# A hybrid decoder step on one core: conv gate columns last, parts split in place, taps held back in the memory projection, a paced layer norm

## The chip, the cores and the metric

The kernel runs on one core of one Trainium2 chip. The metric is device time in microseconds (us), the median of several runs; one further execution was taken with the hardware profiler. A difference of under about 2% between two kernels is called "same". Engines are named as in the profile: PE is the matmul engine, PEld its weight loads, DVE the vector engine, ACT the scalar engine, POOL the general engine, SP the engine whose queue issues all of this kernel's DMAs.

## The reference

One layer for two groups with the same weights: a prompt (1 sequence of 1024 tokens) and samples (8 sequences of 8 tokens with earlier state). All in float32, d_model 2048.

```python
def hybrid_layer(x, ...):
    proj = jnp.einsum("bld,de->ble", x, w_in)
    glu_a, glu_b, conv_gate, qkv, dn_gate, beta_in, decay_in, mem_q, mem_gate = jnp.split(proj, splits, axis=-1)

    u = glu_a * jax.nn.sigmoid(glu_b)                                   # conv group, 512 channels
    hc, conv_state = causal_dwconv(u, conv_prev, conv_w)                # width 31
    hc = layer_norm(hc + conv_b.astype(dt), conv_ln_g, conv_ln_b)
    out_conv = (jax.nn.silu(hc) * jax.nn.silu(conv_gate)).astype(dt)

    qkv_c, qkv_state = causal_dwconv(qkv, qkv_prev, qkv_conv_w)         # deltanet group, 8 heads of 128
    ...
    o, s_final = gated_delta_rule(q, k, v, g, beta, s0)
    ...
    scores = jnp.einsum("blhd,bmhd->bhlm", mq, mem_k.astype(dt)).astype(f32) * (MEM_HEAD_DIM ** -0.5)
    p = jax.nn.softmax(scores, axis=-1).astype(dt)                      # memory group, 4 heads of 128, 256 tokens
    om = jnp.einsum("blhm,bmhd->blhd", p, mem_v.astype(dt)).reshape(b, l, MEM_WIDTH)
    out_mem = (om * jax.nn.silu(mem_gate)).astype(dt)

    mixed = jnp.concatenate([out_conv, out_dn, out_mem], axis=-1)
    h = jnp.einsum("ble,ed->bld", mixed, w_out)
    y = layer_norm(DEEPNORM_ALPHA * x + h, ln_g, ln_b)
    return y, conv_state, qkv_state, s_final
```

The prompt's memory keys and values are themselves projected from `mem_prompt` (256 x 2048) with `w_mem_k` and `w_mem_v`; the samples bring cached ones.

## The kernel before, in words

**Precision.** Every large matmul is done in three: an operand is split into a high part (rounded to FP32R by an ACT copy) and a low part (DVE: operand minus high part), and `mm3` adds high x high, high x low and low x high. `split_quarter` does this for the weights, a piece of 128 x 512 at a time: ACT writes `wh`, DVE writes `wl`, each from 4 rotating buffers; `ensure(2)` keeps two pieces split ahead of PE in program order. So every piece of weights needs one ACT copy and one DVE subtraction before PE can use it. `put_mixed` (L570) does the same for each finished 128-channel block of the mixed output and writes both parts to DRAM.

**Stages.** Pass 0 takes the first 512 prompt tokens and the 64 sample tokens (moving sizes 288 + 288), pass 1 the other 512 prompt tokens. Each pass runs over 52 columns of `w_in` (128 channels each, `gemm`): 96 matmuls a column in pass 0, 48 in pass 1. `ct_order` gives their order: 32 columns of the deltanet group head by head, eight of the GLU (a and b by turns), then four conv gates (columns 40 to 43), four memory queries (44 to 47), four memory gates (48 to 51). In pass 0, before column 44, `run_mem` projects the memory: 192 matmuls, 32 pieces of weights and 8 of the memory (`load_mem`) to split. In pass 1 `reload_mem` reads the keys and values back at the same column. Then the output phase: `mixed` times `w_out` in blocks of 16 pieces of weights, four column blocks for the first half (`g` = 0, five token tiles, 14 matmuls a piece) and four for the second (`g` = 1, four tiles, 12 matmuls a piece); the last block is cut in two.

**Side work.** Everything else is written as generators (`gen_k`, `gen_chain`, `gen_s`, `gen_cgroup`, `gen_cln`, `gen_att`, `gen_ln` ...). `Side.tick` is called between the matmuls of a column (after every four calls of `mm3`, in pass 1 after every two), in the projection and in the output phase once a piece, and moves each generator on by a step when the planner's clocks (`Model`, one for each engine) say that the tiles it waits for are ready. The program order on each engine is fixed by this planner when the kernel is built; on the chip each engine then goes through its instructions in that order. `Side.drain` calls `tick` until a condition holds, with no column matmuls between. A generator that yields "B" is put off to the next tick.

**Room.** Side work takes its tiles from a pool of 20 `W` tiles; `room(n)` puts a generator off until `n` are free, and `need()` drains until one is. The eviction of a gate column (`gate` in `finish`) calls `need()` and holds its tile until the product that uses it. `gen_att` takes three tiles for a head, and in pass 0 five more for the sample group, whose cached keys and values it loads (`kts`, `vts`). `gen_att` waits for the head before it and, at the end, for its gate.

**The conv group.** `gen_cgroup` (L1020) makes `u` = a x sigmoid(b) and then the 31 taps on DVE, one or two instructions a tap (prompt, samples); a tap waits while the planner's DVE clock is over 1200 ns ahead of its PE clock (L1062). Once all four channel blocks are done, `gen_cln` does the layer norm over channels: sums on POOL, two sums over partitions on PE, then for each block a product with `rstd`, Silu, the product with the gate (it waits for `("g", j)`) and `put_mixed`.

**The end.** After 13 pieces of the first output block `open_out` drains all side work, closes the work pool and opens the pool of the output phase: eight `y` tiles, six `xt`, the layer norm's weights. `residual` (DVE) evicts a bank after each block, `gen_ln` takes statistics after each block and, after the fourth, normalises in four chunks: ACT scales and shifts, DVE multiplies by `lng` and adds `lnb`, SP writes the chunk. After the first block of the second half a drain of all side work (L1689) makes sure that the first half's layer norm is written out before its `y` buffers are taken again.

All recorded operations go through the one helper line 88 (`Proxy`), so the profile's groups are told apart by their tiles: `m` is a column's result, `mm` the memory projection's, `om` the output phase's (and a head's output), `ps` side work on PE, `hc` the conv taps and layer norm, `smz` and `pt` the softmax, `held` the last six pieces of `w_out`.

## Time and profile before

| what | value |
|---|---|
| runs | 4051.27, 2019.34, 2021.03 us; median 2021.03 |
| profiled execution, own time | 2022.13 us |
| its span (first to last instruction) | 2020.4 us |
| mean granted PE clock | 0.992 |
| PE busy | 1964.0 us, 97% |
| DVE busy | 1374.2 us, 68% |
| ACT busy | 922.5 us, 46% |
| conv taps: first of pass 0, last of pass 1 | 585.8 us, 1526 us |
| memory projection, first to last matmul | 715 to 764 us |

The prediction quotes four kinds of views. A *page* line gives an engine's busy time; its row of 40 digits cuts the span in 40 slices (9 is 90% or more). The *waits* say which engine's which tile waited for whom: us in total, how often, the longest. A *stretch* row gives start:end, length, then busy time and instructions of the engines, the granted PE clock, the DMA share and GB/s; a stretch asked for one tile alone counts that tile's instructions only. The *order of time* gives start, duration, engine, operation, output <- inputs, how many were merged, and in brackets the idle time before it and whom it waited for.

### The profile page before, as it was taken

What the parts mean: (1) busy time and instruction counts of PE and PEld (TensorE: products, weight loads), DVE (VectorE), ACT (ScalarE), POOL (GpSimd) and SP (SyncE); (2) the same over time, 40 slices, a digit from 0 to 9 for tenths busy, and PEclk for the clock granted to TensorE, in tenths of its full rate; (3) what the DMA queues carried; (4) which work ended last, traced back from release to release, by engine and by line L of the source; (5) the groups of instructions that cost most, each with busy time, mean ns of one, the idle gap of its engine ahead of it and who ended that gap; (6) DMA issues with size and microseconds to landing.
All of it is one profiled execution on the core that took longest, in us unless ns stands there. A gap on an engine that the chain in (4) does not pass through costs nothing.

```text
span 2020.4 us, 33329 instructions
## 1 busy us (share of the span) xinstructions
PE 1964.0 (97%) x12172; PEld 1710.7 (85%) x12172; DVE 1374.2 (68%) x3423; ACT 922.5 (46%) x2279; POOL 159.9 (8%) x345
## 2 busy tenths in 40 slices
PE   8999999999999999899999999999999999999995
PEld 7999999999999979877888878888887788887784
DVE  6677767866878896455767777778995433338447
ACT  6555555555543244466545544553324522215124
POOL 6111101101101001000000000000101000000001
PEclk9999999999999999999999999999999999999998
DMA  6232333233323354374333333333332493376444
GB/s 209 85 110 74 100 110 110 73 102 110 102 95 101 99 183 131 110 231 150 120 97 99 100 99 106 110 100 95 101 115 77 139 375 103 102 245 206 140 132 150
DMA packets 114294, 257.35 MB, mean 127 GB/s; under 512 B 35281, under 2 KB 39633, under 8 KB 113873
## 3 DMA queue, kind: packets, MB, share of 16 engines
q1 hardware_dynamic: 114128, 255.22, 39.2%
q8 instruction: 96, 1.57, 0.3%
q14 instruction: 70, 0.57, 0.1%
HBM read 219.15 MB, written 36.01 MB: 126 GB/s over the span
## 4 chain that ended last, share of the span: by engine, by line
PE 44%; DVE 6%; issue 1%; ACT 1%; DMA 1%; SPq 0%; POOL 0%; DVEq 0%; ACTq 0%
PE m L88 22%; PE om L88 17%; PE ps L88 5%; DVE y L88 2%; DVE hc L88 1%; DVE wl L88 1%; DVE cv L88 1%; SPq L88 0%; DMA vts<-in_cv_dram 0%; ACT wh L88 0%; DMA ysc<-Y 0%; DVE held L88 0%; DMA mx<-mxl 0%; DMA out_y_p_dram<-y 0%; ACT gmh L88 0%
## 5 line engine op out<-in xcount | busy, mean ns | idle before, releaser
L88 PE MATMUL m<-x,wh 128*128 128x288 f32 (+1 forms) x4992 | 1228.1, 335 | 7.8 <-ACT wh L88 7.8
L88 PEld LDWEIGHTS m<-x,wh 128*128 128x128 f32 x4992 | 833.0, 189 | 84.2 <-issue 16.7
L88 PE MATMUL m<-x,wl 128*128 128x288 f32 (+1 forms) x2496 | 818.4, 328 | 1.7 <-DVE wl L88 1.7
L88 DVE TENSOR_TENSOR wl<-raw,wh 128x512 fp32r<-128x512 f32 x586 | 405.2, 698 | 294.5 <-ACT wh L88 285.6
L88 ACT CAST wh<-raw 128x512 fp32r<-128x512 f32 x586 | 357.3, 620 | 374.3 <-PE om L88 228.2
L88 PEld LDWEIGHTS m<-x,wl 128*128 128x128 f32 x2496 | 470.0, 188 | 37.4 <-DVE wl L88 2.9
L88 PE MATMUL om<-wh,x 128*128 128x512 f32 x1064 | 335.0, 391 | 0.0
L88 PEld LDWEIGHTS om<-wh,x 128*128 128x128 f32 x1064 | 200.7, 189 | 42.7 <-issue 1.0
L88 PE MATMUL om<-wl,x 128*128 128x512 f32 x564 | 220.8, 391 | 3.8 <-DVE wl L88 3.8
L88 DVE SCALAR_TENSOR_TENSOR hc<-u,cvc,hc 128x512 f32<-128x512 f32 x360 | 200.7, 595 | 2.4
L88 DVE TENSOR_TENSOR xt<-mb,X 128x8 f32<-128x8 f32 (+30 forms) x496 | 136.9, 276 | 10.5
L88 DVE SCALAR_TENSOR_TENSOR cv<-xr,qcw,cv 128x512 f32<-128x512 f32 (+1 forms) x216 | 128.9, 597 | 7.7
L88 PEld LDWEIGHTS om<-wl,x 128*128 128x128 f32 x564 | 106.5, 189 | 26.4 <-DVE wl L88 4.4
L88 ACT ACT_TABLE_LOAD x83 | 106.5, 1283 | 44.2 <-DVE smz L88 30.1
L88 DVE TENSOR_REDUCE X<-xt 128x4 f32<-128x8 f32 (+30 forms) x496 | 110.2, 222 | 10.6
L88 ACT ACTIVATE oi<-ps,GT 128x128 f32<-128x128 f32 x56 | 20.6, 368 | 210.1 <-DVE r L88 207.7
L88 ACT ACTIVATE jk<-ps 128x128 f32<-128x128 f32 x128 | 33.3, 275 | 51.8 <-PE ps L88 51.7
L88 ACT COPY xr<-m 128x288 f32<-128x288 f32 (+3 forms) x96 | 33.3, 396 | 20.5 <-PE m L88 20.0
L88 ACT ACTIVATE cv<-cv 128x512 f32<-128x512 f32 x48 | 30.3, 631 | 19.5 <-DVE cv L88 19.2
L88 PEld LDWEIGHTS ps<-S,cv 128*128 128x128 f32 x224 | 32.0, 190 | 4.7 <-DVE S L88 2.2
L88 PE MATMUL ps<-S,cv 128*128 128x128 f32 x224 | 34.4, 276 | 1.1 <-DVE S L88 1.1
L88 DVE SCALAR_TENSOR_TENSOR y<-xt,om 128x512 f32<-128x512 f32 (+1 forms) x36 | 24.2, 682 | 16.4 <-PE om L88 13.7
(318 smaller groups left out, 1817.4 us busy)
## 6 DMA issues: line engine op xcount, KB each, us to landing
raw<-in_wt_dram SPq DMA_DIRECT2D x208, 512.0 KB, 3.8
raw<-in_wo_dram SPq DMA_DIRECT2D x72, 512.0 KB, 3.9
x<-mx SPq DMA_DIRECT2D x16, 576.0 KB, 8.2
mb<-ysc SPq DMA_DIRECT2D x128, 64.0 KB, 2.2
mx<-mxh SPq DMA_DIRECT2D x32, 256.0 KB, 4.8
mx<-mxl SPq DMA_DIRECT2D x32, 256.0 KB, 4.9
xt<-in_xp_dram SPq DMA_DIRECT2D x32, 256.0 KB, 4.4
x<-mx SPq DMA_DIRECT2D x16, 512.0 KB, 3.6
```

Of the source, the lines that this page charges most:

```text
L88: r = fn(**kw)
```

## The change

1. `ct_order`: the four conv gate columns go to the end of each pass (columns 48 to 51); memory queries are now 40 to 43, memory gates 44 to 47. The memory projection and its loads (pass 0) and `reload_mem` (pass 1) move from column 44 to column 40.
2. `put_mixed`: the low part is written over the input tile; one new tile in place of two.
3. The limit by which taps may run ahead of PE becomes a variable: 1200 ns as before, but -500 while `run_mem` puts out its matmuls.
4. `gen_ln`: each chunk's two DVE instructions wait while the planner's DVE clock is over 1200 ns ahead of PE.
5. After the first block of the second half the drain waits only for the first token tile's `gen_ln` of the first half, not for all side work.

```diff
@@ ct_order
-    order += [COL_CGATE + j for j in range(4)]
     order += [COL_MQ + j for j in range(4)]
     order += [COL_MGATE + j for j in range(4)]
+    order += [COL_CGATE + j for j in range(4)]
@@ the order of loads, the column loops of both passes
-        if t == 44:
+        if t == 40:
@@ put_mixed
         yield (m,)
-        yield from room(2)
-        parts = [W([P, NTOK[p]], F32R, name=n, held=True) for n in ("mxh", "mxl")]
-        act.copy(out=parts[0], in_=m)
-        dve.tensor_tensor(out=parts[1], in0=m, in1=parts[0].bitcast(F32), op=ALU.subtract)
-        fr()
-        yield tuple(parts)
+        yield from room(1)
+        hi = W([P, NTOK[p]], F32R, name="mxh", held=True)
+        act.copy(out=hi, in_=m)
+        parts = (hi, m.bitcast(F32R))
+        dve.tensor_tensor(out=parts[1], in0=m, in1=hi.bitcast(F32), op=ALU.subtract)
+        yield (hi, m)
@@ gen_cgroup
+    ahead = [1200]
-            while md.clk["DVE"] > md.clk["PE"] + 1200:
+            while md.clk["DVE"] > md.clk["PE"] + ahead[0]:
                 yield "B"
@@ run_mem
+        ahead[0] = -500
         for i in range(8):
             if i % 2 and i < 7:
                 load_mem()
...
+        ahead[0] = 1200
         need(4)
@@ the pass 0 loop
-        fin = gemm(0, t, fin, refill_b if t == 51 else (lambda q: load_mem() if q == 2 else None) if t == 43 else None)
+        fin = gemm(0, t, fin, refill_b if t == 51 else (lambda q: load_mem() if q == 2 else None) if t == 39 else None)
@@ gen_ln
             act.activation(out=yc, in_=yc, func=AF.Identity, scale=r, bias=nmr)
             yield
+            while md.clk["DVE"] > md.clk["PE"] + 1200:
+                yield "B"
             dve.tensor_tensor(out=yc, in0=yc, in1=gc, op=ALU.mult)
@@ the output phase
             if g and cb == 0:
-                side.drain(lambda: side.q)
+                side.drain(lambda: any(e[0] is first for e in side.q))
...
                     side.add(gen_ln(P, cb, st, ys[i], bst[i], O["y_p"][g * 512 + o:g * 512 + o + P, :]))
+                    if i == 0:
+                        first = side.q[-1][0]
```

## The prediction, as it was put on record

> **What bounds the kernel now.** I read the page first, then the waits of PE, then stretches of 50 us, then the order of time around each stretch that has a hole. The page says that PE is busy nearly all the time at nearly the full clock:

> ```profile
> PE 1964.0 (97%) x12172; PEld 1710.7 (85%) x12172; DVE 1374.2 (68%) x3423; ACT 922.5 (46%) x2279; POOL 159.9 (8%) x345
> PE   8999999999999999899999999999999999999995
> PEclk9999999999999999999999999999999999999998
> ```

> Of the 2020.4 us of the span, 56.4 are without a matmul. A good part lies in the start and the tail (the 8 and the 5 at the row's ends), which the change leaves alone or only reorders. What is left is in the waits of PE (us in total, times, longest):

> ```profile
> PE ps L88 <- DVE pt L88: 6.8, 4, 3.2
> PE om L88 <- DVE wl L88: 3.8, 1, 3.8
> PE ps L88 <- DVE ut L88: 3.4, 5, 1.4
> PE mm L88 <- DVE wl L88: 3.0, 3, 1.4
> PE om L88 <- DVE held L88: 2.6, 3, 1.0
> PE ps L88 <- DMA kts<-in_ckT_dram: 1.5, 2, 0.9
> ```

> No edit takes a matmul away, so the change can only win back waits, and what follows from a wait. That second thing is seen in the stretches (length, then busy time of PE, PEld, DVE, ACT, POOL, then granted clock):

> ```profile
> 800.00:850.00 50.00, 44.65 (x312) 40.30 (x311) 20.30 (x30) 20.82 (x35) 4.28 (x3) 0.93 0.35 111
> 1550.00:1600.00 50.00, 46.83 (x195) 36.19 (x193) 23.44 (x43) 25.88 (x52) 3.88 (x3) 0.93 0.19 63
> 1650.00:1700.00 50.00, 50.00 (x221) 40.95 (x220) 17.51 (x27) 10.56 (x17) 0.00 (x0) 1.00 0.51 171
> 1850.00:1900.00 50.00, 46.25 (x193) 37.74 (x192) 31.44 (x50) 14.31 (x23) 0.00 (x0) 0.93 0.56 178
> ```

> The three stretches with a hole of over 2.5 us have a clock of 0.93; an undisturbed one has 1.00. A mean of 0.93 over 50 us is 0.07 x 50 = 3.4 us of work lost to half speed, on top of the wait itself. So each long wait costs its length plus about 3.4 us.

> **Part 1: gate columns last, memory projection at column 40.** The hole at 840, PE in order of time, with the one ACT row that matters:

> ```profile
> 835.66 1.20 PE L88 MATMUL ps<-kts,dgq 128*32 128x256 f32 x4 [0.58 <-DMA kts<-in_ckT_dram]
> 837.82 1.74 PE L88 MATMUL ps<-kts,dgq 128*32 128x256 f32 x12 [0.95 <-DMA kts<-in_ckT_dram]
> 842.79 0.66 PE L88 MATMUL ps<-ident,pt 128*128 128x128 f32 x2 [3.23 <-DVE pt L88]
> 843.96 1.94 PE L88 MATMUL ps<-vts,ptm 128*32 128x256 f32 x16 [0.52 <-DVE ptm L88]
> 846.71 0.69 PE L88 MATMUL m<-x,wh 128*128 128x288 f32 x2
> 851.94 0.42 PE L88 MATMUL m<-x,wh 128*128 128x288 f32 x2
> 840.29 1.28 ACT L88 ACT_TABLE_LOAD   x1 [8.22 <-DVE smz L88]
> ```

> Scores, softmax and values of one head follow each other with no column's matmul between. I read that as a drain: the eviction of a memory gate asks for a tile (`need` in `gate`), none of the 20 W tiles is free, and the planner puts out side work until one is. By the code, 16 tiles are then held by things that wait: four conv gates, four conv outputs, four memory queries, four tiles of memory keys and values; a head of the sample group needs up to five more. Waits: 0.58 + 0.95 + 3.23 + 0.52 = 5.3; with the clock (0.69 against 0.42 for the same pair of matmuls) 3.4 more: 8.7 us. With the gates last, four of the 16 aren't there when the first heads run, and the heads begin four columns earlier, under eleven columns in place of seven. I count the 8.7 as won. The pass 1 hole:

> ```profile
> 1580.47 1.11 PE L88 MATMUL ps<-ident,pt 128*128 128x128 f32 x4 [2.71 <-DVE pt L88]
> 1582.04 3.78 PE L88 MATMUL ps<-PT,mvs 128*128 128x512 f32 x4 [0.46 <-ACT PT L88]
> ```

> Same pattern, without sample work: 2.71 + 0.46 + 3.4 = 6.6 us. In the new order what ends last in pass 1 is the conv layer norm's product with its gate, the split and the DMAs, which hold no matmul; PE meanwhile has the first output block. Won: 6.6. The loads that move (16 of the projection's weights, four of the memory, in pass 1 four reloads of keys and values; the heads' loads of cached keys and values behind them) go through SP in the order of their users, and the weight loads queue behind them by the same number as before, only at another column: 0.

> [...]

> **Part 2: taps held during the projection.** The wait of PE for `wl` at 734:

> ```profile
> 729.90 2.66 DVE L88 SCALAR_TENSOR_TENSOR hc<-u,cvc,hc 128x512 f32<-128x512 f32 x6
> 732.48 1.29 DVE L88 TENSOR_TENSOR ml<-raw,mh 128x512 fp32r<-128x512 f32 x2
> 733.68 1.89 DVE L88 TENSOR_TENSOR wl<-raw,wh 128x512 fp32r<-128x512 f32 x3
> 734.42 0.50 PE L88 MATMUL mm<-wl,mh 128*128 128x512 f32 x1 [1.43 <-DVE wl L88]
> ```

> Six taps and two splits of the memory stand in DVE's queue ahead of the split that PE waits for; taps allowed 1.2 us ahead of PE become taps at least 0.5 us behind it. Six taps are 2.66 us and the wait was 1.43, so dropping half of them covers it: 3.0 us won over the three waits. The taps move on, and here is what DVE has for them (first two rows: taps alone; then all of DVE and PE in the same stretches):

> ```profile
> 715.00:763.00 48.00, 25.97 (x57) 0.00 (x0) 1.00 0.59 194
> 1465.00:1509.00 44.00, 34.44 (x46) 0.00 (x0) 1.00 0.37 120
> 1509.00:1526.00 17.00, 7.19 (x10) 0.00 (x0) 1.00 0.22 73
> ...
> 715.00:763.00 48.00, 45.01 (x193) 35.55 (x192) 46.60 (x94) 22.88 (x39) 0.00 (x0) 1.00 0.59 194
> 1465.00:1509.00 44.00, 44.00 (x196) 36.44 (x195) 43.01 (x63) 12.12 (x21) 1.46 (x1) 1.00 0.37 120
> ```

> In the projection DVE has 46.60 - 25.97 = 20.6 us of other work in 48, so some 27 us are free and taps still get part of them; whatever is put off, at most 26 us, lands under the eleven columns behind it, where PE runs through a full DVE without a wait (1465 to 1509: DVE 43.01 of 44, PE 44.00 of 44). Cost 0 while that holds.

> **Part 3: layer norm paced, and a drain for one tile alone.** DVE, then PE, at the end of the first block of the second half:

> ```profile
> 1861.12 0.68 DVE L88 TENSOR_TENSOR wl<-raw,wh 128x512 fp32r<-128x512 f32 x1
> 1861.72 0.68 DVE L88 TENSOR_TENSOR y<-y,lng 128x512 f32<-128x512 f32 x1
> ...
> 1867.74 0.68 DVE L88 TENSOR_TENSOR y<-y,lnb 64x512 f32<-64x512 f32 x1
> 1868.35 2.47 DVE L88 SCALAR_TENSOR_TENSOR y<-xt,om 128x512 f32<-128x512 f32 x4
> 1870.74 1.28 DVE L88 TENSOR_TENSOR wl<-raw,wh 128x512 fp32r<-128x512 f32 x2
> ...
> 1871.47 0.79 PE L88 MATMUL om<-wl,x 128*128 128x512 f32 x1 [3.75 <-DVE wl L88]
> ```

> From 1861.72 to 1868.35, 6.6 us of layer norm lie between two splits, then 2.5 of residuals. PE has two split pieces in hand, 2 x 12 matmuls x 50/221 us = 5.4. The change cuts most of the 6.6: with 1.3 of it left (one step of two instructions), 1.3 + 2.5 = 3.8 is under 5.4, and the wait is gone: 3.75 + 3.4 = 7.2 us. The ninth `y` tile takes the first tile's buffer; its residual on DVE would wait for that tile's last DMA with the splits behind it. That tile has first turn in every tick, so I take 0; if it is late, a DMA's few us come back, at most the 7.2. At the tail the same pacing may let the `held` splits through earlier (2.6 of wait), but the two tiles' layer norm then lies between PE's end and the last rows on DVE: 0, bounds -2.6 and +2.6.

> **Part 4: the parts split in place.** One W tile less at 32 places. In place, the instruction costs what it costs out of place (0.68 at 1861.72 against 0.68 at 1861.12), the DMAs are the same. A head that waited for two tiles starts its split with one; that moves side work by some us and shuffles the short waits of the delta rule, of which `ut` is the largest with 3.4 in all. 0, bounds -3.4 and +3.4.

> **Sum.** 8.7 + 6.6 + 3.0 + 7.2 = 25.5. Back goes what eight heads under new neighbours and one paced block may wait: the short waits here are 0.46 to 0.58 us, so 7 of them, 3.5. Net 22.0. The profiled execution took 2022.1 (span 2020.4 and 1.7 around it), 1.1 over the median of the runs shown, 2021.0. So 2021.0 - 22.0 = **1999.0**.

> **Rivals.**

> The waits move: heads now run beside taps, so a softmax step on DVE stands behind up to 1.2 us of them, and ACT's table load (1.28) is as before. For it: both large holes are softmax waits. Against: a wait needs a drain, or a planner that is over 1 us off. Then parts 2 and 3 alone pay: 2021.0 - 10.2 = 2010.8, say 2008 to 2018.

> The conv layer norm comes too late (the other side). DVE work of the heads now precedes pass 1's last taps, 34.44 + 7.19 = 41.6 us of them from 1465 on:

> ```profile
> L88 DVE TENSOR_REDUCE smz<-ps 128x2 f32<-128x512 f32 x8 | 5.5, 689 | 3.3 <-PE ps L88 3.3
> L88 DVE TENSOR_SCALAR pt<-pt,smz 128x256 f32<-128x256 f32 x16 | 4.9, 351 | 0.4
> ...
> 1567.67 0.68 DVE L88 TENSOR_TENSOR hc<-hc,rstd 128x512 f32<-128x512 f32 x1
> ```

> These 10.4 us would delay the taps from 1526 to about 1540. From the last tap to the first product with `rstd` it took 1567.7 - 1526 = 42 us. The output phase closes the work pool after 13 pieces of its first block, 13 x 14 x 50/221 = 41 us after column 51 (about 1603), and drains. If the taps end later than 1603, the whole 42 us fall into that drain; PE has 2 x 14 x 50/221 = 6.3 in hand, so 36 + 3.4 come back: 2021.0 - 25.5 + 39 = 2034.5. 1540 is 63 us short of that point.

> The room still runs out: the gates' tiles go, but the queries and gates of the memory heads pile up behind taps that were put off. Then the pass ends keep 15.3 and parts 2 and 3 give part of theirs: 2013 to 2022.

> **How the numbers follow.** Forecast (1988 to 2008) 0.62; waits move 0.18; room runs out 0.10; layer norm late 0.06; better still, with `held` and the delta rule's waits gone (2021.0 - 25.5 - 2.6 - 3.4 = 1989.5, and below) 0.04. The range 1988 to 2018 takes in the bounds of the forecast, the moved waits and half of the third case: about 0.83. Within 2% (40 us, about what can be told from no change) lie all cases but their far ends: faster by more needs 1980.6, which is under the sum with everything won, 0.02; slower by more needs 2061, more than the late layer norm costs, 0.02; same 0.96.

> **What would show it.** Right: clock 1.00 in the stretches near 840, 1580 and 1870; no wait of PE for `pt` over 1 us; none for `wl` in `mm` over 0.5; pass 0's last `vts` matmul earlier than before; layer norm rows between all splits of the second half. Wrong: a hole over 2.5 us anywhere in the new trace with a clock of 0.93 in its stretch, above all at the thirteenth piece of the output phase, or a PE total that waits less while the span stays.

## The result, and the profile after

| | before | after |
|---|---|---|
| runs, us | 4051.27, 2019.34, 2021.03, 2017.98 | 2001.15, 1999.54, 2002.81, 2000.63 |
| median | 2020.18 | 2000.89 |
| profiled execution, own time | 2022.13 | 2001.15 |
| its span | 2020.4 | 1999.4 |
| mean granted PE clock | 0.992 | 0.996 |

The ratio of after to before is 0.9913, with a 95% interval of 0.9897 to 0.9928 (the run of 4051.27 us is left out of it): the kernel is 15 to 21 us faster. The forecast was 1999.0, the median is 2000.89. Faster, then, but by less than the 2% that the prediction named as the bound of what can be told.

The page of after, as it answers to the first fence of the prediction:

```profile
PE 1953.0 (98%) x12172; PEld 1705.7 (85%) x12172; DVE 1373.3 (69%) x3423; ACT 923.1 (46%) x2280; POOL 164.2 (8%) x345
PE   8999999999999999999999999999999999999995
PEclk9999999999999999999999999999999999999998
```

The same 12172 matmuls keep PE busy for 11.0 us less (1964.0 before): they ran at the full clock more of the time (before has three stretches of 6.83 us at half clock between its start and its tail, which is 10.2 us lost; after has none). And the span less the busy time fell from 56.4 to 46.4, so 10.0 us of waits are gone. 11.0 + 10.0 are the 21.0 us of the span. The forecast, sorted in the same way, had 10.2 of clock and 15.2 of waits (5.3 + 3.17 + 3.0 + 3.75), less 3.5 that come back: 21.9. DVE, ACT and their counts hardly moved: no work went away.

The waits of PE in after (us in total, times, longest):

```profile
PE m L88 <- ACT wh L88: 8.8, 2, 7.5
PE ps L88 <- DVE ut L88: 3.8, 7, 1.4
PE om L88 <- DVE held L88: 2.6, 3, 1.0
PE om L88 <- DVE wl L88: 2.3, 1, 2.3
...
PE ps L88 <- DVE ptm L88: 1.4, 1, 1.4
...
PE ps L88 <- DVE pt L88: 0.6, 2, 0.3
```

The softmax wait `pt` fell from 6.8 to 0.6, longest 0.3. The line for `mm` is gone altogether. The wait for `wl` in the output phase is still there, 2.3 in place of 3.8. The 7.5 of the first line is the start of the kernel; the other wait in it, 1.39 us, is new, and `ptm` grew from 0.5 to 1.4. The short waits of the delta rule (`ut`) are 3.8, against 3.4 before.

The stretches (length, busy time of PE, PEld, DVE, ACT, POOL, then granted clock):

```profile
650.00:700.00 50.00, 49.86 (x258) 42.38 (x258) 47.86 (x96) 23.50 (x41) 0.00 (x0) 1.00 0.67 215
800.00:850.00 50.00, 49.76 (x369) 45.96 (x366) 30.23 (x64) 25.20 (x52) 7.13 (x4) 1.00 0.37 118
850.00:900.00 50.00, 47.19 (x344) 39.91 (x343) 33.62 (x55) 33.92 (x60) 3.22 (x4) 1.00 0.67 207
900.00:950.00 50.00, 48.61 (x237) 38.87 (x236) 28.80 (x65) 31.91 (x72) 2.97 (x8) 1.00 0.46 142
1550.00:1600.00 50.00, 50.00 (x220) 41.03 (x219) 27.70 (x41) 24.34 (x39) 3.94 (x3) 1.00 0.61 199
1850.00:1900.00 50.00, 47.69 (x211) 39.13 (x210) 24.71 (x40) 11.22 (x18) 0.00 (x0) 1.00 0.52 163
```

All three stretches that had 0.93 have 1.00. At 1550 to 1600 nothing is lost any more. At 800 to 850, 5.35 of loss became 0.24, but 850 to 950 now loses 2.81 + 1.39 (before 0.16 + 1.09), and 1850 to 1900 still 2.31. Three waits are most of it: 1.41, 1.39 and 2.31; the rest are short. The first two, in order of time (start, duration, engine, operation, in brackets the idle time before it):

```profile
871.12 1.28 ACT L88 ACT_TABLE_LOAD   x1
873.01 0.68 ACT L88 CAST mxh<-hc 128x576 fp32r<-128x576 f32 x1
873.72 0.76 DVE L88 TENSOR_TENSOR hc<-hc,mxh 128x576 fp32r<-128x576 f32 x1 [1.89 <-ACT mxh L88]
875.67 0.42 DVE L88 COPY ptm<-ps 128x256 f32<-128x256 f32 x1
876.14 1.07 PE L88 MATMUL ps<-vts,ptm 128*32 128x256 f32 x16 [1.41 <-DVE ptm L88]
...
908.31 1.28 ACT L88 ACT_TABLE_LOAD   x1 [2.39 <-DVE g L88]
909.86 1.28 ACT L88 ACT_TABLE_LOAD   x1
911.41 1.28 ACT L88 ACT_TABLE_LOAD   x1
914.28 0.61 ACT L88 CAST wh<-raw 128x512 fp32r<-128x512 f32 x1
914.94 0.73 PE L88 MATMUL m<-x,wh 128*128 128x512 f32 x2 [1.39 <-ACT wh L88]
```

At 876 the last head of pass 0 wants its transposed probabilities, and the copy of them stands in DVE's queue behind the split of a conv block, which waits 1.89 us for ACT, which has just loaded a table (1.28) and has a product's gate (`sgate`, 0.71) ahead of it. At 915 the three table loads of pass 1's delta gates stand in ACT's queue ahead of a weight copy. Neither wait halves the clock here (1.00 from 850 to 950).

### The profile page after: what moved, and what is told of

It is laid out like the page before. It is cut to its first block, busy times and chain, and to the rows that moved or that the text cites. A ratio compares the mean times of both kernels' runs of the same rounds, so it can differ in the third digit from the quotient of the medians.

```text
span 1999.4 us, 33302 instructions
## 1 busy us (share of the span) xinstructions
PE 1953.0 (98%) x12172; PEld 1705.7 (85%) x12172; DVE 1373.3 (69%) x3423; ACT 923.1 (46%) x2280; POOL 164.2 (8%) x345
## 4 chain that ended last, share of the span: by engine, by line
PE 83%; DVE 9%; ACT 4%; DMA 2%; issue 1%; SPq 0%; POOL 0%; DVEq 0%; ACTq 0%
PE m L88 53%; PE om L88 17%; PE ps L88 11%; DVE wl L88 2%; DVE cv L88 2%; PE mm L88 2%; DVE y L88 1%; DVE hc L88 1%; ACT L88 1%; ACT wh L88 1%; DVE xt L88 1%; DMA raw<-in_wt_dram 1%; DVE x L88 0%; DVE X L88 0%; DVE S L88 0%
## 5 line engine op out<-in xcount | busy, mean ns | idle before, releaser
L88 PE MATMUL m<-x,wh 128*128 128x288 f32 (+1 forms) x4992 | 1228.5, 335 | 9.1 <-ACT wh L88 8.8
L88 PEld LDWEIGHTS m<-x,wh 128*128 128x128 f32 x4992 | 831.6, 189 | 86.2 <-issue 15.0
L88 PE MATMUL m<-x,wl 128*128 128x288 f32 (+1 forms) x2496 | 817.4, 327 | 1.3 <-DVE wl L88 1.3
L88 DVE TENSOR_TENSOR wl<-raw,wh 128x512 fp32r<-128x512 f32 x586 | 403.1, 694 | 276.6 <-ACT wh L88 268.0
L88 ACT CAST wh<-raw 128x512 fp32r<-128x512 f32 x586 | 357.2, 620 | 326.5 <-PE om L88 229.2
L88 PEld LDWEIGHTS m<-x,wl 128*128 128x128 f32 x2496 | 469.2, 188 | 36.8 <-DVE wl L88 2.4
L88 PE MATMUL om<-wh,x 128*128 128x512 f32 x1064 | 333.4, 390 | 0.0
L88 PEld LDWEIGHTS om<-wh,x 128*128 128x128 f32 x1064 | 199.4, 188 | 42.2 <-issue 1.0
L88 PE MATMUL om<-wl,x 128*128 128x512 f32 x564 | 219.6, 389 | 2.3 <-DVE wl L88 2.3
L88 DVE SCALAR_TENSOR_TENSOR hc<-u,cvc,hc 128x512 f32<-128x512 f32 x360 | 199.9, 592 | 2.2
L88 DVE TENSOR_TENSOR xt<-mb,X 128x8 f32<-128x8 f32 (+30 forms) x496 | 136.9, 276 | 10.4
L88 DVE SCALAR_TENSOR_TENSOR cv<-xr,qcw,cv 128x512 f32<-128x512 f32 (+1 forms) x216 | 128.9, 597 | 7.7
L88 PEld LDWEIGHTS om<-wl,x 128*128 128x128 f32 x564 | 105.9, 188 | 24.9 <-DVE wl L88 2.9
L88 ACT ACTIVATE oi<-ps,GT 128x128 f32<-128x128 f32 x56 | 20.6, 368 | 214.2 <-DVE r L88 212.0
L88 DVE TENSOR_REDUCE X<-xt 128x4 f32<-128x8 f32 (+30 forms) x496 | 110.1, 222 | 10.6
L88 ACT ACTIVATE jk<-ps 128x128 f32<-128x128 f32 x128 | 33.5, 275 | 52.0 <-PE ps L88 51.9
L88 ACT COPY xr<-m 128x288 f32<-128x288 f32 (+3 forms) x96 | 33.4, 397 | 19.1 <-PE m L88 18.9
L88 ACT ACTIVATE cv<-cv 128x512 f32<-128x512 f32 x48 | 30.3, 630 | 22.2 <-DVE cv L88 21.7
L88 PEld LDWEIGHTS ps<-S,cv 128*128 128x128 f32 x224 | 31.9, 190 | 5.5 <-DVE S L88 3.2
L88 DVE SCALAR_TENSOR_TENSOR y<-xt,om 128x512 f32<-128x512 f32 (+1 forms) x36 | 24.2, 683 | 17.6 <-PE om L88 16.5
L88 PE MATMUL ps<-S,cv 128*128 128x128 f32 x224 | 34.4, 276 | 1.7 <-DVE S L88 1.7
```

The costliest lines, as they stand in the source:

```text
L88: r = fn(**kw)
```

## The experiments

Each kernel is after or before with one edit. The times are medians; each ratio is against the kernel before, run beside it on the same chip, whose median was 2019.6 to 2021.3. An interval is 0.0009 to 0.0017 to either side, 2 to 3 us; after's own ratio lies 0.0008 above the quotient of its medians, so what an edit to after costs comes out up to 3 us apart by medians and by ratios. The worths below go by medians, the profiled spans stand beside them, and what is under 3 us is read from the traces alone.

**The order undone.** After, with columns, loads and projection where they stood before.

```diff
+    order += [COL_CGATE + j for j in range(4)]
     order += [COL_MQ + j for j in range(4)]
     order += [COL_MGATE + j for j in range(4)]
-    order += [COL_CGATE + j for j in range(4)]
...
-        if t == 40:
+        if t == 44:
```

> The changed kernel with the old order of columns (gates at 40 to 43, projection at 44); the other parts of the change stay. The forecast's theory, that the order closes the two holes at the pass ends: both holes return as waits of PE for pt of over 2.5 us, the granted clock is 0.93 in their 50 us, and the time is 2001 + 15 = 2016 us (2012 to 2020). The rival, that the tile saved by the split in place made the room: no hole over 1.5 us, clock 1.00, 2000 to 2006 us.

2013.69 us, ratio 0.9962 [0.9948, 0.9977]: the order is worth 12.8 us in company of the other parts (12.2 by the spans, 2011.6 against 1999.4; 9.9 by the ratios). But the hole at 840 did not come back where it was. PE in order of time:

```profile
868.70 0.63 PE L88 MATMUL ps<-ident,pt 128*128 128x128 f32 x4 [1.76 <-DVE pt L88]
879.36 0.63 PE L88 MATMUL ps<-ident,pt 128*128 128x128 f32 x4 [3.21 <-DVE pt L88]
892.23 1.05 PE L88 MATMUL bd<-raw,wbr 128*32 128x512 f32 x4 [2.72 <-DMA raw<-in_xb_dram]
...
950.93 0.66 PE L88 MATMUL ps<-ident,cv 128*128 128x128 f32 x4 [2.32 <-ACT cv L88]
```

The holes lie 30 to 110 us later, at the end of pass 0 and in pass 1's first column, and amount to more: 1.76 + 3.21 + 2.72 + 2.32 = 10.0. And the hole of pass 1 at 1580 did not return: PE is busy for 50.00 of the 50 us from 1550. So that hole does not hang on the order alone; in the runs below it also goes with held taps alone and with more tiles alone. What they have in common, a change of pace of the side work before it, is my reading.

**The order alone.** Before, with part 1 and nothing else (the edit of the last kernel, the other way round).

> The kernel before with the new order of columns alone. The order's theory: 2020 - 15.3 = 2005 us (2001 to 2009), no softmax wait over 1 us at the pass ends, the layer norm's wait of 3.7 us with its half clock and the 3 us of the projection still there. The rival, that order and saved tile are needed together: a hole over 2.5 us at a pass end remains, 2010 to 2020 us.

2012.82 us, ratio 0.9960 [0.9945, 0.9974], 7.9 us by the medians. Both pass-end holes are gone (longest `pt` 0.6), and two others are there in full, the stretch of the projection and that of the output phase:

```profile
650.00:700.00 50.00, 45.91 (x241) 39.04 (x240) 49.71 (x103) 21.42 (x38) 2.16 (x6) 0.99 0.58 186
...
1850.00:1900.00 50.00, 46.24 (x193) 37.74 (x192) 25.95 (x41) 11.41 (x19) 0.00 (x0) 0.93 0.51 163
```

With the order alone, the projection's waits grow from 3.0 to 4.1, DVE is at 49.71 of 50 in that stretch, and the longest wait, 2.31 us, is followed by 3.41 us at half clock (0.99 and 0.98 over the stretches from 650 to 700 and from 700 to 750). Shorter waits also come in place of the hole at 840: from 800 to 950 PE is without a matmul for 5.0 us, against 6.6 before, though that hole was 5.3 of the 6.6. The time lies in the rival's range, but not for its reason: no hole is left at a pass end.

**Taps free again.** After, with 1200 in place of -500 during the projection.

```diff
-        ahead[0] = -500
+        ahead[0] = 1200
```

> The changed kernel with taps allowed 1200 ns ahead during the projection as well. The forecast's theory: the waits of PE for wl in the projection return with about 3 us (1.5 at most for one), time 2001 + 3 = 2004 us. The rival, that holding taps back only moves their load behind the projection: the waits return there but the later ones (1.4 us on a head's ptm at 875, 1.4 us on a weight piece at 914) shrink by as much, 1999 to 2002 us.

2009.78 us, ratio 0.9944 [0.9929, 0.9959]. Holding the taps is worth 8.9 us by the medians, 8.3 by the spans (2007.7), 6.3 by the ratios: two to three times the forecast. PE in the projection:

```profile
694.04 0.40 PE L88 MATMUL mm<-wh,mh 128*128 128x512 f32 x1
696.71 0.65 PE L88 MATMUL mm<-wl,mh 128*128 128x512 f32 x1 [2.28 <-DVE wl L88]
697.16 0.63 PE L88 MATMUL mm<-wh,ml 128*128 128x512 f32 x1
...
699.72 0.63 PE L88 MATMUL mm<-wh,ml 128*128 128x512 f32 x1
700.15 0.47 PE L88 MATMUL mm<-wh,mh 128*128 128x512 f32 x1
700.46 0.40 PE L88 MATMUL mm<-wl,mh 128*128 128x512 f32 x1
```

The same kind of instruction takes 0.63 in place of 0.40 for some 3.4 us behind the wait: half clock, seen matmul by matmul. The three waits are 4.0, the half clock costs 1.7 (0.97 over 650 to 700), and from 800 to 950 PE is busy for 143.3 us in place of 145.6. Together 8.0 of the 8.3 us between the spans. The time is above both expectations. The rival, that the free taps would only shift the waits and give them back later, falls: those later waits are longer too, not shorter. Why they are is not shown.

**Holding alone.** Before, with part 2 and nothing else.

> The kernel before with the taps held back during the projection and nothing else. The forecast priced this part at 3.0 us in the old order: the three waits of PE for wl (1.43, 1.26, 0.31) go, no other changes, 2017 to 2018 us. The rival from the run with free taps in the new order (8.9 us lost): the holding itself is worth about 8 us, 2011 to 2014 us. A third way: taps put off meet the gates and heads of the old order, and the time is that of before or more, 2020 to 2026 us.

2018.03 us, ratio 0.9986 [0.9977, 0.9995]: 1.6 us by the medians, 2.8 by the ratio, against the 3.0 of the forecast. Of the projection's waits, 3.0 before, 0.75 is left. But "no other changes" was wrong: the holes at 840 and 1580 are gone here as well, and come back as those of the first experiment: 1.72, 3.19, 2.83 and 2.32 us at 868, 877, 889 and 950.

**No taps at all during the projection.** After, with a limit that lets no tap through there.

```diff
-        ahead[0] = -500
+        ahead[0] = -10**6
```

> The changed kernel with no conv tap at all put out during the projection (limit one millisecond behind PE in place of 0.5 us). If what the holding wins is the waits inside the projection alone: these are gone already, so the time is that of the changed kernel or worse by what the later taps cost, 2001 to 2008 us. If the taps put off cost nothing behind the projection (the forecast's 0): 2000 to 2002 us. If the fewer taps the better: under 1999 us.

2000.7 us, ratio 0.9902 [0.9887, 0.9917]: the same time as after. Put-off taps cost nothing that these runs can measure, as the forecast took it, even when all of them are put off.

**Layer norm and drain alone.** Before, with part 3 and nothing else.

> The kernel before with the paced layer norm and the drain for one tile, nothing else. The forecast: the wait of 3.75 and its half clock go, 2020.7 - 7.2 = 2013.5 us. The rival from the runs that undo half of this part (3.6 us each): a wait of about 2 us for the residual behind the tile's last DMA stays, with no half clock or a short one, 2016 to 2018 us.

2017.62 us, ratio 0.9990 [0.9980, 0.9999]: 2.0 us where 7.2 were forecast. The wait for `wl` is 1.85 in place of 3.75, still with 3.41 us at half clock behind it (0.97 at 1850 to 1900); the holes at 840 (1.51 and 3.23) and 1577 (2.71) are there as before.

**Each half of part 3 undone.** After without the pacing, and after with the drain of all side work:

```diff
-            while md.clk["DVE"] > md.clk["PE"] + 1200:
-                yield "B"
```

> The changed kernel without the pacing in the layer norm; the drain still waits for the first tile alone. If the burst of layer norm ahead of the splits made the wait: PE's wait for wl at the end of the first block of the second half is 3.7 us again with clock 0.93 in its stretch, 2001 + 4.8 = 2006 us. If the full drain made it: wait at 2.3 us or under, clock 1.00, 2000 to 2002 us.

```diff
-                side.drain(lambda: any(e[0] is first for e in side.q))
+                side.drain(lambda: side.q)
```

> The changed kernel with the full drain as before, pacing kept. If the full drain puts the burst back: a wait for wl of 3.7 us or more and the half clock, 2006 us or more. If pacing alone spreads the burst: wait at 2.3 us, 2000 to 2002 us.

2004.59 us, 0.9918 [0.9903, 0.9932], and 2004.40, 0.9918 [0.9901, 0.9934]. Both intervals overlap that of after, so the traces decide (spans 2001.7 and 2002.5, 2.3 and 3.1 over after): in both the old wait stands there again, 3.73 and 3.75 us. The output phase's stretch, without the pacing and then with the full drain:

```profile
1850.00:1900.00 50.00, 46.27 (x199) 37.94 (x198) 24.04 (x38) 10.28 (x17) 0.00 (x0) 0.97 0.50 154
```

```profile
1850.00:1900.00 50.00, 46.25 (x197) 37.78 (x196) 23.87 (x38) 10.60 (x17) 0.00 (x0) 0.97 0.50 156
```

One half without the other leaves the wait as long as it was. And the clock is 0.97 in both, where before and the order alone had 0.93 behind a wait of the same length; the expectations had taken the price of before.

**The splits ahead of the residuals.** What is left in after at 1850, in order of time:

```profile
1844.15 0.67 DVE L88 TENSOR_TENSOR wl<-raw,wh 128x512 fp32r<-128x512 f32 x1
1844.76 0.68 DVE L88 TENSOR_TENSOR y<-y,lng 128x512 f32<-128x512 f32 x1
...
1846.29 0.53 SPq L88 DMA_DIRECT2D out_y_p_dram<-y  x1
...
1848.13 0.69 DVE L88 TENSOR_TENSOR y<-y,lnb 128x512 f32<-128x512 f32 x1
1848.74 1.88 DVE L88 SCALAR_TENSOR_TENSOR y<-xt,om 128x512 f32<-128x512 f32 x3
1851.73 0.69 DVE L88 SCALAR_TENSOR_TENSOR y<-xt,om 128x512 f32<-128x512 f32 x1 [1.11 <-issue]
1852.33 1.28 DVE L88 TENSOR_TENSOR wl<-raw,wh 128x512 fp32r<-128x512 f32 x2
1853.07 0.50 PE L88 MATMUL om<-wl,x 128*128 128x512 f32 x1 [2.31 <-DVE wl L88]
```

Six instructions of layer norm (4.0 us) and four residuals lie between two splits, and ahead of the fourth residual, the one of the ninth `y` tile, DVE stands for 1.11 us. The row names no releaser, but the trace's semaphore events do: DVE's queue holds on a semaphore until 1851.68, and what raises it is the output DMA issued at 1846.29, which lands at 1851.65, 5.4 us after its issue. So this is the last DMA of the buffer which that tile takes; the prediction had that case as "if it is late". The splits stand behind it. So: put two more pieces' splits ahead of the residuals.

```diff
             if g and cb == 0:
                 side.drain(lambda: any(e[0] is first for e in side.q))
+            if g and cb == 0:
+                ensure(4)
```

> The changed kernel with one edit more: at the end of the first block of the second half, two more pieces of weights are split ahead of the residuals (ensure(4)). Reading of the trace after: the fourth residual on DVE waits 1.1 us for the first tile's last output DMA and the splits stand behind it, so PE's wait of 2.31 us goes to under 0.5 and the time to about 1998.7 us. The rival, that the residuals just wait as long behind the splits and the wait moves one piece on: 2000 to 2002 us.

1998.83 us, ratio 0.9890 [0.9876, 0.9905]; the profiled span is 1997.5, 1.9 under that of after. DVE and then the stretch:

```profile
1844.86 0.68 DVE L88 TENSOR_TENSOR wl<-raw,wh 128x512 fp32r<-128x512 f32 x1
...
1849.44 1.28 DVE L88 TENSOR_TENSOR wl<-raw,wh 128x512 fp32r<-128x512 f32 x2
1850.64 2.47 DVE L88 SCALAR_TENSOR_TENSOR y<-xt,om 128x512 f32<-128x512 f32 x4
```

```profile
1850.00:1900.00 50.00, 50.00 (x222) 41.43 (x221) 25.58 (x41) 11.43 (x19) 0.00 (x0) 1.00 0.57 173
```

PE's wait is gone, and so is DVE's: all four residuals run without a break, now that they come 1.9 us later (in after the output DMA lands at 1851.65; the fourth residual starts here at 1852.43). This is the fastest of all kernels here; its interval overlaps that of after, so the 2 us are shown by the trace, not by the times.

**Room alone.** Before, with two more `W` tiles, paid for with one buffer of raw weights. If the hole at 840 is a drain for want of tiles, it must go.

```diff
-    rawp = ctx.enter_context(tc.tile_pool(name="rawp", bufs=5))
+    rawp = ctx.enter_context(tc.tile_pool(name="rawp", bufs=4))
...
-    NW, NX, NU, N5, NZ = 20, 1, 2, 17, 12
+    NW, NX, NU, N5, NZ = 22, 1, 2, 17, 12
```

> The kernel before with 22 W tiles in place of 20, paid for with one raw weight buffer of five; order and all else as before. If the holes at the pass ends come from the lack of a W tile (the forecast's reading): the hole at 840 shrinks below 2.5 us and its stretch has clock 1.00, perhaps the one at 1580 too, 2004 to 2014 us. If they come from softmax chains with too little cover whatever the room: both stay, 2018 to 2022 us. If the fifth raw buffer matters, new waits of PE for wh or wl with a DMA behind them, over 2020 us.

2022.19 us, ratio 1.0009 [0.9999, 1.0018]: nothing won. Both holes are gone from their places (800 to 850 and 1550 to 1600 have PE at 50.00 of 50, clock 1.00), so want of tiles did set where they lay. New ones stand in pass 1's first columns:

```profile
922.35 1.28 ACT L88 ACT_TABLE_LOAD   x1 [1.66 <-issue]
925.22 1.22 PE L88 MATMUL m<-x,wh 128*128 128x512 f32 x2 [3.21 <-ACT wh L88]
...
967.13 0.09 DVE L703 MEMSET mb<- 128x32 f32 x1 [2.93 <-DMA mb<-ysc]
971.25 0.64 PE L88 MATMUL m<-x,wl 128*128 128x512 f32 x1 [2.19 <-DVE wl L88]
```

A head's softmax, put off over the pass's end, takes ACT for a table load (922) just behind the gates' three; DVE waits 2.93 us for a small DMA of the delta rule with a weight split behind it (967). I read this as columns that are short, not tiles: the heads begin too late in pass 0. One reservation: the raw buffer given up may have a part in these waits; that wasn't separated.

**The split in place undone.** After, with the `put_mixed` of before (two tiles).

> The changed kernel with put_mixed as before (two new tiles, input freed). The forecast's theory, part 4 is worth 0 with bounds of 3.4 either way: 1998 to 2005 us, clock 1.00 in all stretches. The rival, that the saved tile is what keeps the pass ends from a drain: a hole over 2.5 us with clock 0.93 at a pass end, 2008 us or more.

2002.25 us, ratio 0.9909 [0.9894, 0.9923], span 2000.3 against 1999.4: no difference that these runs can measure. The wait at the end of the second half's first block is 2.10 us here, 2.31 in after, and the mean clock of the profiled execution is 0.996 in both.

**More turns for the other side work.** The kernel with the splits ahead, and in it a yield in `put_mixed` between the ACT copy and the DVE subtraction and three in pass 1's gates, against the two waits of 1.4 us.

```diff
         act.copy(out=hi, in_=m)
+        yield (hi,)
...
```

> The kernel with the splits ahead of the residuals, and more places at which the planner may put other work between: in put_mixed between ACT's copy and DVE's subtraction, in pass 1's gates after the Exp, before the product with the reciprocal and before the last ACT copy. If the waits of 1.4 us at 875 (a DVE copy behind a subtraction that waits for ACT) and at 914 (a weight copy on ACT behind a chain of three table loads) come from order on these queues: both fall under 0.5, 1998.8 - 2.5 = 1996 us. If they only move: 1998 to 2000 us.

2000.99 us, ratio 0.9904 [0.9890, 0.9919], span 1999.7 against 1997.5 without these yields: above both expectations. Both waits are gone, and a longer one is there in their place:

```profile
908.09 1.92 PE L88 MATMUL bd<-raw,wbr 128*32 128x512 f32 x4 [2.99 <-DMA raw<-in_xb_dram]
```

It comes with 6.83 us at half clock (0.93 at 900 to 950). Two waits of 1.4 that left the clock alone were the better bargain.

## Why the prediction was right, and which terms were not

**What bounds the kernel: right.** No work went away, and the 21 us are waits and clock in nearly equal parts, as the sum had them (10.2 of clock, and 15.2 of waits less the 3.5 that come back). Of its signs, the clock of 1.00 in the three stretches, the short waits for `pt`, none for `wl` in `mm` and the earlier `vts` all came.

**Part 1, forecast 15.3.** The holes at 840 and 1580 went, as the prediction said. The size was off in two ways. Alone, the order gives 7.9, since the projection's waits grow and take a half clock with them, and shorter waits come in place of the hole at 840; in company it is worth 9.9 (ratios) to 12.8 (medians). And the 6.6 for the hole at 1580 don't belong to the order alone: that hole goes with the order, but also with held taps alone and with more tiles alone, and doesn't return with the old order. The step "I read that as a drain: ... none of the 20 W tiles is free" holds for the place of the hole, not for its price: with tiles to spare, the same heads run late and wait in pass 1's first columns. What the new order gives them is time: the `vts` matmuls of pass 0's heads ran from 844 to 974.5 before and run from 760 to 877 now.

**Part 2, forecast 3.0.** Right for the kernel before as far as these runs tell (1.6 by the medians, 2.8 by the ratio, 2.3 of the projection's waits), too small for the kernel after: 8.9 (6.3 by the ratios). The prediction costed it "over the three waits" of the old trace. But part 1 moves the projection to right behind the GLU columns, and there the free taps make waits of 4.0 with a half clock and lengthen those of the pass end. The taps are no denser there (24.0 of 44 us, against 26.0 of 48 in the old place); the trace of that run has, ahead of the wait of 2.28, four taps and then the first steps of the next conv block in a row. The sum of the parts was made part by part; taken alone the three give 0.40%, 0.14% and 0.10% by their ratios, 0.64% together, and the change gives 0.87%. The intervals alone would leave room for equality; the waits at the projection, 3.0 in the old order and 4.0 with a half clock in the new, do not. The put-off taps cost 0, as said.

**Part 3, forecast 7.2.** This term was too large. At its place 3.75 of wait and 3.4 of clock became 2.31 of wait, which is 4.8 in these two executions (in others such a wait may cost clock as well: behind the 1.85 us of layer norm alone and of no taps at all the stretch has 0.97); undoing either half costs 2.3 to 3.7, by spans or medians. Two steps failed. "With 1.3 of it left (one step of two instructions)": 4.0 are left, three steps; by the code, the drain for the first tile lets other tiles' steps through as well, which no run separates. And "that tile has first turn in every tick, so I take 0; if it is late, a DMA's few us come back": it is late, by 1.11 us. With the splits moved ahead of both, the wait is gone. The traces tell the two apart: in the six kernels in which DVE stands at this place, PE's wait less DVE's is 1.2 each time (2.31 - 1.11 in after, 2.10 - 0.92, 1.89 - 0.67, 1.87 - 0.69, 1.85 - 0.67 and 1.85 - 0.65 in others), so 1.2 are the layer norm's steps and residuals, and the rest is the late DMA. The tail's `held` stayed at 2.6, the 0 that was taken.

**Part 4, forecast 0.** Right within what can be measured.

**What comes back, 3.5.** The new waits of 1.41 and 1.39, and the 2.31 which is part 3's miss. The first two are of the kind that the first rival feared (a head's step behind other work on DVE, a table load on ACT), and neither touched the clock.

**The rivals.** The late conv layer norm didn't come. Its taps (first row: instructions, shortest, median and longest in ns, first and last start) end where the prediction had put them, at about 1540. The last product with the gate starts at 1598.3; the output phase starts at 1595.7 here, so its thirteenth piece, 41 us later by the prediction's sum, comes at about 1637, and PE is busy for 50.00 of the 50 us from 1600. (In before the output phase starts at 1612.7, so the prediction's 1603 was too early a point, on the safe side.)

```profile
L88 DVE SCALAR_TENSOR_TENSOR hc<-u,cvc,hc x9: 744/750/752, 1535.0 to 1542.7; 128x512 f32<-128x512 f32 x9
...
L88 DVE TENSOR_TENSOR hc<-hc,sgate x4: 684/692/693, 1572.0 to 1598.3; 128x512 f32<-128x512 f32 x4
```

The prediction had put the moved waits at 2008 and more, and the room that runs out at 2013 and more. Too small a part 2 and too large parts 1 and 3 nearly cancelled: the total was better than its terms, and that part is luck.

**The clock's price.** "Each long wait costs its length plus about 3.4 us" was read from three holes of before, each with 6.83 us at half clock, and was right for these three. It isn't a rule. Of the six waits of 3.73 to 3.75 us at this same place (before, and five of the experiments), three cost 3.4 (0.93 at 1850 to 1900) and three cost 1.7 (0.97). So it is luck as well that the 10.2 us of clock in the sum are the 10.2 that the two profiled executions differ by; what sets the price was not shown, and the last section has only a reading of it.

## What to carry to other kernels

Where several edits change the order of one queue, cost each in the order that the others make, not in the old trace: here the held taps were worth about twice as much or more once the projection had moved next to them. Where in-order queues carry the splits that PE lives on, look at what stands ahead of each split and what that waits for, an output DMA of a reused buffer among them; split a piece or two more ahead of such a place. A drain for want of buffers shows where a stall lies; before buying buffers, ask whether the work has enough independent matmuls left to run under. And one profiled execution gives one price of a wait in clock: take it as one of several.

## What the runs showed of the hardware

In the two traces of before and after the changes of the clock lie on equal steps: in before the three falls ahead of the tail, at 842.86, 1580.14 and 1870.27, lie 243, 459 and 544 times 3.4133 us after 13.42, where the record of the clock begins, and each half clock lasts two such steps; in after the one fall, at 1985.19 in the tail, lies 578 steps after 12.28. In the step right before these three falls PE was busy for 0.18, 1.03 and 0.86 of the 3.41 us. The 2.31 us of after lie across two steps, with a boundary at 1852.07; PE was busy for 2.10 us of the one and 2.42 of the other, and the clock stayed at 1.00.

My reading of this, an estimate that no run tests, is that a wait's price hangs on where it falls on these steps. They lie differently in each execution (the record begins at 13.42 in before and at 12.28 in after), so the price would belong to the execution more than to the kernel. The 19 executions of the kernel before that ran beside the last experiments fit this: their spans go from 2015.0 to 2021.9 us, their mean clocks from 0.995 to 0.991. It was read from the traces afterwards, where PE's instructions overlap one another (0.40 us long and 0.23 apart at 690 with the taps free), so the busy times carry some error.
